# Products of the identity with itself behind the last value product of two head mixers

## The chip, the cores and the metric

The kernel runs on one core of a Trainium2 chip. The metric is the device time of one execution, in microseconds (us). Beside the median of several runs there is one profiled execution, whose trace gives the start and the length of every instruction on TensorE (PE; its weight loads are PEld), VectorE (DVE), ScalarE (ACT) and GpSimd (POOL), and the clock that was granted to TensorE: 1.00 stands for 2.4 GHz and 0.50 for 1.2 GHz.

## The reference, cut to what matters

Three layers run one behind another over 256 tokens of 1024 channels. Each layer has a mixer and a gated feed-forward part with a short convolution, and each of the two halves is entered through a modulated norm and left through a gated residual.

```python
for i in range(DEPTH):                       # two layers; a third has a mixer of its own
    sh1, sc1, g1, sh2, sc2, g2 = split(silu(c) @ ada_w[i] + ada_b[i])
    h = rms_norm(x, norm_mix[i]) * (1 + sc1) + sh1
    mix = stick_breaking_attention(h, ...) if i == 0 else dsa_attention(h, ...)
    x = x + g1 * mix
    h = rms_norm(x, norm_ffn[i]) * (1 + sc2) + sh2
    x = x + g2 * conv_ffn(h, ...)
...
o = einsum('bhqs,bshd->bqhd', a, v)          # the value product of a mixer, 16 heads of 64
return o.reshape(B, S, 1024) @ w_out         # and the product with its output weights
```

The change touches the end of the first two mixers: the value products of the last heads and what follows, the product with `w_out`, the residual and the entry into the feed-forward part.

## The kernel before, in words

All activations stand transposed, channels on the 128 partitions and 256 tokens along the free axis, in eight tiles of 128 channels. Large products are done in three terms: weights and activations are each split into a rounded part (`wh`, `xh`, `oh`) and a rest (`wl`, `xl`, `ol`), and `three` (L306) issues high times high, high times low and low times high into one PSUM bank. For weights, ScalarE makes `wh` (L412) out of the loaded `raw` and VectorE the rest `wl` (L424).

A mixer runs its heads as a background generator (`heads_in_flight`) between the pieces of the large products. For two heads at a time, `product(h)` issues a chain of four fp32 matmuls with 64 output columns (`po<-a,V` in the first mixer, `po<-pT,U` in the second); then `split_later` has ScalarE round the result to `oh` (L339) and VectorE subtract for `ol` (L340). The sixteen heads give eight channel tiles `k` of `oh` and `ol`.

`output` then multiplies by `w_out`. It goes through the first six tiles with `down`, as they come ready, and through the last two with `down_last`, which finishes the output tiles `m` in the order 0, 2, 4, 6, 1, 3, 5, 7. The eight output tiles share four `acc` banks, two to a bank: 0 and 1 share one, 2 and 3 the next. When an output tile is finished, `residual` has VectorE add it to `x` (L705, `x<-acc,mod,x`), ScalarE make the next half's `xh` out of it (L700), VectorE the rest `xl` (L701), and ScalarE and VectorE gather the squares for the next norm (`sq`, L650 and L731). The sums of squares are matmuls with a column of ones (`po<-ones,sq`). Between these stand VectorE's row products for the modulation of later layers (`ada_one`, L544, 1.2 us each), which wait for their weights `adaw` from memory, and, behind all of them, `opening`, the first product of the feed-forward part.

The order on each engine is set by a scheduler that simulates the program; a dependency without a semaphore (`behind`) ties one instruction behind another. `busy` (L897) issues fp32 products of a 128x128 tile of minus ones with itself into the `small` PSUM bank, read by nobody; the kernel before calls it three times at the start of the program (18, 8 and 8 products), and nowhere else.

In what follows, **the first place** is the end of the first mixer (`stick`, from 137 to 158 us of the span) and **the second place** the end of the second mixer (`sparse`, from 467 to 484 us).

Of the kernel before, what the change touches and what calls it, by code (L numbers as in the profile page):

```python
# [273 lines left out]
class Prog:  # L274
# [312 lines left out]
    def gate(self, L, h, k):  # L587
        return self.M[L][:, 6 * h + 4 + k // 4, k % 4:k % 4 + 1]
# [305 lines left out]
        nc.scalar.activation(self.ident_r, self.ident, AF.Copy)  # L894
        return p

    def busy(self, n):  # L897

        b = self.bank("small")
        for _ in range(n):  # L900
            self.mmul(b[:, 0:128], self.negones, self.negones, start=True, stop=True)

    def pin(self, mark):
        last = {}
# [121 lines left out]
    def stick(self, outer):  # L1026
        nc = self.nc
        with ExitStack() as es:
            pool = lambda name, bufs: es.enter_context(self.tc.tile_pool(name=name, bufs=bufs, reuse_waits="tile"))
            sv = pool("sbv", 3)  # L1030
            V = sv.tile([128, 2, D], F32, name="V", bufs=1)
            qk, ready, st = {}, set(), {}

            def value(i):
                def fn(u, b):
                    c = i * 512 + u * 256
                    nc.scalar.activation(V[:, :, c:c + 256], b, AF.Copy)
                return fn

            def heads(g):  # L1040
                def fn(u, b):
                    if u == 0:
                        qk[g] = sv.tile([128, 4, T], F32, name="qk")
                    nc.scalar.activation(qk[g][:, 2 * u:2 * u + 2], b, AF.Copy, scale=(0.125, 1.0)[u])
                    if u:
                        ready.add(g)
                return fn

            Z, S, E, PO = {}, {}, {}, {}

            def strict(w):

                d = w.rearrange("p (a t) -> p a t", a=3)[:, 0:3:2, :]
                return nc.gpsimd.affine_select(d, d, pattern=[[0, 2], [1, 128]], base=-1, channel_multiplier=-1,
                                               compare_op=ALU.is_ge, fill=0.0).ins

            def scores(h0, n):
                for h in range(h0, h0 + n):
                    Z[h] = self.score_bank(h, st)
                chain = []  # L1060
                for i, j in ((i, j) for i in range(2) for j in reversed(range(n))):
                    h = h0 + j
                    r = slice(h % 2 * 64, h % 2 * 64 + 64)
                    q, k = qk[h // 4][r, h % 4 // 2], qk[h // 4][r, 2 + h % 4 // 2]
                    chain.append(self.mmul(Z[h][:, i * 256:256 + i * 128], k[:, i * 128:i * 128 + 128], q[:, i * 128:256],
                                           start=i == 0))
                self.chained(chain)
                for h in range(h0, h0 + n):
                    soft(h)

            def soft(h):
                z = Z[h]
                e = sp.tile([128, 384], F32, name="e")
                nc.scalar.activation(e, z[:, :384], AF.Abs)
                self.act(e, e, AF.Exp, scale=-1.0)
                self.act(e, e, AF.Ln, bias=1.0)
                S[h] = sp.tile([128, 384], F32, name="s", bufs=4)

                def fn():
                    nc.vector.scalar_tensor_tensor(S[h], z[:, :384], 0.0, e, op0=ALU.max, op1=ALU.add)  # L1080
                    strict(S[h])
                self.after(1, fn)

            def suffix(h):
                z, s = Z.pop(h), S.pop(h)
                self.mmul(z[:, 0:256], self.nu, s[:, 0:256])
                self.mmul(z[:, 128:256], self.negones, s[:, 256:384])
                self.mmul(z[:, 256:384], self.nu, s[:, 256:384], stop=True)
                E[h] = sp.tile([128, 384], F32, name="a", bufs=WP + 1)
                self.act(E[h], z[:, :384], AF.Exp)  # L1090
                strict(E[h])

            def product(h):
                if h % 4 == 0:
                    PO[h // 4] = self.bank("po")
                o = PO[h // 4][:, h % 4 // 2 * 256:h % 4 // 2 * 256 + 256]
                a = [E.pop(h), E.pop(h + 1)]
                chain = []
                for t in range(2):
                    for i in (1, 0):  # L1100
                        r, c = slice(i * 64, i * 64 + 64), slice((h + i) * 64, (h + i) * 64 + 64)
                        chain.append(self.mmul(o[r, t * 128:256], V[:, t, c], a[i][:, t * 256:256 + t * 128],
                                               t == 0 and h % 4 == 0, t == 1))
                self.chained(chain)
                st["split"] += 1
                self.split_later(oh[:, h // 2], ol[:, h // 2], o,
                                 lambda: st.update(ready=h + 2, split=st["split"] - 1))

            self.start([value(0), heads(0), heads(1), value(1)], V, sv)
            sk, sp = pool("sbk", 1), pool("sb", 2)  # L1110
            bias = outer.enter_context(self.tc.tile_pool(name="bias", bufs=1, reuse_waits="tile", side="right"))
            bias = bias.tile([128, 16, 256], F32, name="bias")
            self.side.append(self.bias_tables(bias, pool("bk", 1)))
            oh = sk.tile([128, KT, T], F32R, name="oh")
            ol = sk.tile([128, KT, T], F32R, name="ol")
            self.bg.append(self.heads_in_flight(16, st, lambda h: h // 4 in ready, scores, suffix, product, 1, 2, 3))
            self.rate = RS[0]
            for g in (2, 3):
                for u in range(2):
                    self.unit(lambda b, g=g, u=u: heads(g)(u, b))  # L1120
            self.rate = RS[1]
            self.output(oh, ol, st, lambda k: st["ready"] > 2 * k + 1, 0)
            assert not self.side
            return bias

    def output(self, oh, ol, st, need, L, gate=lambda k: None):
        self.flush()
        st["hold"] = True
        while st["open"]:
            self.turnover()  # L1130
            self.advance()
        st["hold"], st["out"] = False, True
        if not LATE:
            self.ada_until(L, 5 if 2 * L + 1 == self.stage else 9)
        self.down_start()
        for k in range(KT - 2):
            while not need(k):
                self.turnover()
                self.advance()
            self.down(oh[:, k], ol[:, k], gate(k))  # L1140
        self.finish_bg()
        self.flush()
        if LATE:
            self.ada_until(L, 5 if 2 * L + 1 == self.stage else 9)
        self.down_last([(oh[:, k], ol[:, k]) for k in range(KT - 2, KT)], self.residual(L, 0))

    def transposed(self, sp, p, b):
# [26 lines left out]
    def sparse(self, bias):  # L1174
        nc, I = self.nc, self.I
        blocks = ((0, slice(0, 128)), (1, slice(128, 384)))
        with ExitStack() as outer:
# [23 lines left out]
            st = {}  # L1201
# [100 lines left out]
            Z, L, E, PO, asked = {}, {}, {}, {}, {}  # L1302
# [36 lines left out]
            def product(h):  # L1339
                if h % 4 == 0:  # L1340
                    PO[h // 4] = self.bank("po")
                o = PO[h // 4][:, h % 4 // 2 * 256:h % 4 // 2 * 256 + 256]
                pT = [E.pop(h), E.pop(h + 1)]
                chain = []
                for t in range(2):
                    for i in (1, 0):
                        r, c = slice(i * 64, i * 64 + 64), slice((h + i) * 64, (h + i) * 64 + 64)
                        rhs = pT[i][:, 128:256] if t else pT[i].rearrange("p (i t) -> p i t", i=3)[:, 0:3:2]
                        chain.append(self.mmul(o[r, t * 128:256], U[:, 1 - t, c], rhs, t == 0 and h % 4 == 0, t == 1))
                self.chained(chain)  # L1350
                st["split"] += 1
                self.split_later(oh[:, h // 2], ol[:, h // 2], o,
                                 lambda: st.update(ready=h + 2, split=st["split"] - 1))

            self.after(1, lambda: self.bg.extend(
                [index(), self.heads_in_flight(16, st, lambda h: h // 4 in ready, scores, turn, product, out_open=3)]))
            for g in range(4):
                if g == 2:
# [390 lines left out]
```

## Time and profile before

| | us |
|---|---|
| median of three runs | 1016.92 |
| lowest and highest of them | 1014.66, 1017.6 |
| the profiled execution | 1016.9 |
| its span, first to last instruction | 1014.9 |
| TensorE busy | 987.1 (97% of the span) |
| VectorE busy | 831.9 (82%) |
| ScalarE busy | 632.6 (62%) |
| mean granted clock of TensorE | 0.994 |

The span and the 2.0 us that lie outside it make the time. TensorE is busy nearly throughout, and by the chain of work that ended last 86% of the span is its. Matmuls overlap in the trace: one of 256 columns lasts 0.28 us while the next begins 0.12 us after it, so that durations of neighbours are not added; what counts is the distance of their starts. A bracket in a timeline row gives how long the engine stood idle before the row and what ended it.

### The profile page before, as it was taken

What the parts mean: (1) busy time and instruction counts of PE and PEld (TensorE: products, weight loads), DVE (VectorE), ACT (ScalarE), POOL (GpSimd) and SP (SyncE); (2) the same over time, 40 slices, a digit from 0 to 9 for tenths busy, and PEclk for the clock granted to TensorE, in tenths of its full rate; (3) what the DMA queues carried; (4) which work ended last, traced back from release to release, by engine and by line L of the source; (5) the groups of instructions that cost most, each with busy time, mean ns of one, the idle gap of its engine ahead of it and who ended that gap; (6) DMA issues with size and microseconds to landing.
All of it is one profiled execution on the core that took longest, in us unless ns stands there. A gap on an engine that the chain in (4) does not pass through costs nothing.

```text
span 1014.9 us, 20080 instructions
## 1 busy us (share of the span) xinstructions
PE 987.1 (97%) x8044; PEld 957.2 (94%) x8044; DVE 831.9 (82%) x1550; ACT 632.6 (62%) x1092; POOL 102.1 (10%) x181
## 2 busy tenths in 40 slices
PE   8999989999999999999999999999999999999997
PEld 8998879999999989988999999999988999999996
DVE  6987698999999899986898899877977689667654
ACT  5585648755554684886875555567785487445543
POOL 0026530011111010110000010100110000000000
PEclk9999999999999999999999999999999999999998
DMA  9999586688988285652668787827670346656531
GB/s 357 405 352 356 184 305 209 209 309 305 313 309 311 108 304 197 233 204 83 231 232 293 268 282 276 288 101 251 250 263 20 126 154 222 224 210 213 203 126 43
DMA packets 45934, 236.71 MB, mean 233 GB/s; under 512 B 5392, under 2 KB 5920, under 8 KB 28176
## 3 DMA queue, kind: packets, MB, share of 16 engines
q1 hardware_dynamic: 26064, 164.73, 44.9%
q0 software_dynamic: 19488, 70.31, 19.6%
q8 instruction: 63, 1.03, 0.4%
q10 hardware_dynamic: 288, 0.39, 0.1%
q14 instruction: 31, 0.25, 0.1%
HBM read 234.33 MB, written 1.07 MB: 232 GB/s over the span
## 4 chain that ended last, share of the span: by engine, by line
PE 86%; DVE 5%; ACT 4%; DMA 4%; issue 1%; SPq 0%; DVEq 0%; POOL 0%; ACTq 0%
PE mm L303 33%; PE acc L303 33%; PE small L303 10%; PE po L303 9%; DVE wl L424 1%; ACT wh L412 1%; DMA adaw<-ada 1%; DVE x L705 1%; DMA raw<-sb 1%; DVE adaw L544 1%; PE acc L1149 1%; DMA raw<-hg 1%; DVE xl L701 1%; DMA raw<-dsa 0%; DMA raw<-ffn 0%
## 5 line engine op out<-in xcount | busy, mean ns | idle before, releaser
L412 ACT ACTIVATE wh<-raw 128x1024 fp32r<-128x1024 f32 x290 | 304.9, 1057 | 255.2 <-PE acc L303 90.2
L424 DVE TENSOR_TENSOR wl<-raw,wh 128x1024 fp32r<-128x1024 f32 x290 | 353.2, 1224 | 92.5 <-ACT wh L412 91.6
L303 PE MATMUL mm<-xl,wh 128*128 128x256 f32 (+1 forms) x872 | 245.7, 283 | 1.2 <-DVE xl L701 1.2
L303 PE MATMUL mm<-xh,wh 128*128 128x256 f32 (+1 forms) x872 | 244.0, 285 | 1.3 <-DVE iv L1684 0.8
L303 PE MATMUL mm<-xh,wl 128*128 128x256 f32 (+1 forms) x872 | 244.6, 283 | 0.0
L544 DVE SCALAR_TENSOR_TENSOR adaw<-adaw,cond 128x1024 f32<-128x1024 f32 x144 | 176.1, 1226 | 6.9 <-DMA adaw<-ada 6.9
L303 PEld LDWEIGHTS mm<-xh,wh 128*128 128x128 f32 x872 | 163.3, 189 | 4.9 <-issue 1.7
L303 PEld LDWEIGHTS mm<-xl,wh 128*128 128x128 f32 x872 | 164.7, 189 | 2.8 <-DVE xl L701 1.8
L303 PEld LDWEIGHTS mm<-xh,wl 128*128 128x128 f32 x872 | 164.1, 189 | 0.2
L303 PE MATMUL acc<-gl,wh 128*128 128x256 f32 x528 | 148.1, 281 | 1.1 <-DVE gl L340 1.1
L303 PE MATMUL acc<-gh,wl 128*128 128x256 f32 x528 | 149.1, 283 | 0.0
L303 PE MATMUL acc<-gh,wh 128*128 128x256 f32 x528 | 148.3, 283 | 0.6 <-DVE x L705 0.6
L537 POOL DMA_DIRECT2D adaw<-ada x125 | 66.5, 532 | 717.2 <-DVE adaw L544 562.0
L303 PEld LDWEIGHTS acc<-gl,wh 128*128 128x128 f32 x528 | 100.3, 190 | 1.3 <-DVE gl L340 1.3
L303 PEld LDWEIGHTS acc<-gh,wh 128*128 128x128 f32 x528 | 98.8, 188 | 0.8 <-DVE x L705 0.8
L303 PEld LDWEIGHTS acc<-gh,wl 128*128 128x128 f32 x528 | 98.9, 187 | 0.0
L303 PE MATMUL small<-xh,wh 128*128 128x256 f32 x240 | 67.7, 282 | 0.0
L303 PE MATMUL small<-xh,wl 128*128 128x256 f32 x240 | 67.6, 282 | 0.0
L303 PE MATMUL small<-xl,wh 128*128 128x256 f32 x240 | 67.4, 281 | 0.0
L303 PE MATMUL acc<-ol,wh 128*128 128x256 f32 x192 | 55.4, 292 | 4.5 <-DVE ol L340 3.7
L303 PE MATMUL acc<-oh,wl 128*128 128x256 f32 x192 | 55.0, 291 | 0.0
L303 PE MATMUL po<-xh,wh 128*128 128x256 f32 x192 | 54.1, 282 | 0.0
(321 smaller groups left out, 2052.2 us busy)
## 6 DMA issues: line engine op xcount, KB each, us to landing
raw<-ffn SPq DMA_DIRECT2D x99, 1024.0 KB, 5.0
adaw<-ada POOLq DMA_DIRECT2D x125, 512.0 KB, 5.3
raw<-dsa SPq DMA_DIRECT2D x15, 1024.0 KB, 5.0
raw<-hg SPq DMA_DIRECT2D x15, 1024.0 KB, 4.9
adaw<-ada SPq DMA_DIRECT2D x19, 512.0 KB, 10.5
raw<-sb SPq DMA_DIRECT2D x16, 512.0 KB, 10.2
raw<-sb SPq DMA_DIRECT2D x8, 1024.0 KB, 8.1
bias<-scr POOLq DMA_DIRECT2D x8, 256.0 KB, 6.9
```

Of the source, the lines that this page charges most:

```text
L303: return self.nc.tensor.matmul(o, a, b, start=start, stop=stop, skip_group_check=True).ins
L412: inst = nc.scalar.activation(h[:, :k * n], self.raws[b][:, c0:c0 + k * n], AF.Copy).ins
L424: inst = nc.vector.tensor_tensor(l[:, :k * n], self.raws[b][:, c0:c0 + k * n], h[:, :k * n], op=ALU.subtract).ins
L537: self.nc.gpsimd.dma_start(raw, self.I[f"ada{L}"][b])
L544: return self.nc.vector.scalar_tensor_tensor(w, w, 1.0, self.cond, op0=ALU.mult, op1=ALU.mult, accum_out=self.M[n // 12][:, n % 12, k:k + ...
L701: return lambda: nc.vector.scalar_tensor_tensor(self.xl[:, m, 0:T], self.x[:, m], a, self.xh[:, m, 0:T], op0=ALU.mult, op1=ALU.subtract)
L705: self.lastx = nc.vector.scalar_tensor_tensor(self.x[:, m], o, self.gate(L, h, m), self.x[:, m], op0=ALU.mult, op1=ALU.add).ins
L1149: self.chained([nc.tensor.transpose(b[:, i * 128:(i + 1) * 128], p[:, i * 128:(i + 1) * 128], self.ident).ins for i in (1, 2, 0)])
```

## The change

`busy` can be given a tile other than the minus ones, and an instruction behind which all of its products are tied. In the first and the second mixer `product` keeps its last matmul in `st["last"]`. `output`, ahead of `down_last`, issues twelve products of the 128x128 fp32 identity with itself in layer 0 and seven in layer 1, tied behind that last matmul. The third mixer keeps no last matmul and gets none.

```diff
-    def busy(self, n):
+    def busy(self, n, w=None, behind=None):
         b = self.bank("small")
+        w = self.negones if w is None else w
         for _ in range(n):
-            self.mmul(b[:, 0:128], self.negones, self.negones, start=True, stop=True)
+            inst = self.mmul(b[:, 0:128], w, w, start=True, stop=True)
+            if behind is not None:
+                self.behind(inst, behind)
...
                 self.chained(chain)
+                st["last"] = chain[-1]
                 st["split"] += 1
...
             self.ada_until(L, 5 if 2 * L + 1 == self.stage else 9)
+        if "last" in st:
+            self.busy((12, 7)[L], self.ident, st["last"])
         self.down_last([(oh[:, k], ol[:, k]) for k in range(KT - 2, KT)], self.residual(L, 0))
```

On TensorE, at the first place, the rows `po<-a,V` are the value product of the last two heads, and `acc<-ol,wh` is the first matmul of `down_last`:

```order
 L303 MATMUL po<-a,V 64x256 x2
 L303 MATMUL po<-a,V 64x128 x2
+L303 MATMUL small<-ident 128x128 x12
 L303 MATMUL acc<-ol,wh 128x256
 L303 MATMUL acc<-oh,wl 128x256
```

The twelve products stand between the two; the order of the products with `w_out` around them is as it was.

On TensorE, at the second place, `mm<-ident,lg` are the transpositions of the last head's weights, `po<-pT,U` the last value product:

```order
 L303 MATMUL acc<-oh,wh 128x256 x4
-L1149 MATMUL mm<-ident,lg 128x128 x3
+L1155 MATMUL mm<-ident,lg 128x128 x3
 L303 MATMUL po<-pT,U 64x256 x2
 L303 MATMUL po<-pT,U 64x128 x2
+L303 MATMUL small<-ident 128x128 x7
 L303 MATMUL acc<-ol,wh 128x256
 L303 MATMUL acc<-oh,wl 128x256
```

Seven products stand there; the two rows with a minus and a plus are the same instruction under another line number.

On VectorE, at the first place, behind the four residuals of output tiles 0, 2, 4 and 6 (`x<-acc,mod_168,x`, L705; `xl`, L701, is the rest for the next half, `sq`, L731, adds up squares). Before:

```order
L705 SCALAR_TENSOR_TENSOR x<-acc,mod_168,x 128x256 x4
L570 TENSOR_TENSOR mod_168<-mod_168,vec 128x4
L701 SCALAR_TENSOR_TENSOR xl<-x,gain_171,xh 128x256 x2
L705 SCALAR_TENSOR_TENSOR x<-acc,mod_168,x 128x256
L701 SCALAR_TENSOR_TENSOR xl<-x,gain_171,xh 128x256 x2
L731 TENSOR_TENSOR sq<-sq 128x512
L705 SCALAR_TENSOR_TENSOR x<-acc,mod_168,x 128x256
L701 SCALAR_TENSOR_TENSOR xl<-x,gain_171,xh 128x256
L705 SCALAR_TENSOR_TENSOR x<-acc,mod_168,x 128x256 x2
L701 SCALAR_TENSOR_TENSOR xl<-x,gain_171,xh 128x256
```

And in the changed kernel, the same stretch of the same engine:

```order
L705 SCALAR_TENSOR_TENSOR x<-acc,mod_168,x 128x256 x4
L570 TENSOR_TENSOR mod_168<-mod_168,vec 128x4
L701 SCALAR_TENSOR_TENSOR xl<-x,gain_171,xh 128x256
L705 SCALAR_TENSOR_TENSOR x<-acc,mod_168,x 128x256
L701 SCALAR_TENSOR_TENSOR xl<-x,gain_171,xh 128x256
L705 SCALAR_TENSOR_TENSOR x<-acc,mod_168,x 128x256
L701 SCALAR_TENSOR_TENSOR xl<-x,gain_171,xh 128x256 x2
L705 SCALAR_TENSOR_TENSOR x<-acc,mod_168,x 128x256
L731 TENSOR_TENSOR sq<-sq 128x512
L705 SCALAR_TENSOR_TENSOR x<-acc,mod_168,x 128x256
```

The residuals of output tiles 1, 3 and 5 move ahead of rests and squares; the instructions are the same. In `opening` behind it, one group of three matmuls on TensorE changes places with two others. Everything else, on VectorE, ScalarE, GpSimd and the DMA queues, stands in the order of before.

## Rows read from the trace of the kernel before

**Rows 1.** The page, part 1: busy us, share of the span, instructions, by engine.

```profile
PE 987.1 (97%) x8044; PEld 957.2 (94%) x8044; DVE 831.9 (82%) x1550; ACT 632.6 (62%) x1092; POOL 102.1 (10%) x181
```

**Rows 2.** Windows at both places: stretch, length, busy by engine, PEclk, DMA share, GB/s.

```profile
139.83:142.70 2.87, 0.00 (x0) 0.00 (x0) 1.49 (x5) 1.06 (x1) 0.72 (x2) 1.00 1.00 368
142.70:142.99 0.29, 0.00 (x0) 0.00 (x0) 0.29 (x2) 0.02 (x1) 0.25 (x1) 0.50 0.88 357
142.99:146.11 3.12, 3.12 (x14) 3.12 (x15) 3.12 (x5) 0.37 (x1) 0.55 (x2) 0.50 0.90 335
146.11:154.32 8.21, 7.99 (x65) 7.57 (x63) 8.21 (x22) 6.13 (x13) 0.79 (x2) 1.00 0.39 133
...
470.38:470.77 0.39, 0.00 (x0) 0.00 (x1) 0.34 (x1) 0.02 (x1) 0.00 (x0) 0.50 0.19 42
470.77:473.79 3.02, 3.02 (x14) 3.02 (x15) 0.42 (x1) 0.36 (x1) 0.00 (x0) 0.50 0.00 0
473.79:479.52 5.73, 5.73 (x47) 5.45 (x46) 5.45 (x14) 4.47 (x11) 0.00 (x0) 1.00 0.00 0
```

**Rows 3.** Timeline of PE, first place: start, length, instructions, idle time before and releaser.

```profile
138.96 0.87 PE L303 MATMUL po<-a,V 128*64 128x256 f32 x8 [1.35 <-POOL a L1054]
142.99 0.58 PE L303 MATMUL acc<-ol,wh 128*128 128x256 f32 x1 [3.17 <-DVE ol L340]
...
147.14 0.39 PE L303 MATMUL acc<-oh,wh 128*128 128x256 f32 x1
...
154.69 0.39 PE L303 MATMUL mm<-xh,wh 128*128 128x258 f32 x1 [0.47 <-ACT wh L412]
...
155.28 0.95 PE L303 MATMUL po<-ones,sq 128*128 128x1 f32 x8
```

**Rows 4.** Timeline of PE, second place.

```profile
467.67 0.55 PE L1149 MATMUL mm<-ident,lg 128*128 128x128 f32 x3 [0.33 <-ACT lg L1329]
469.37 0.87 PE L303 MATMUL po<-pT,U 128*64 128x256 f32 x8 [1.16 <-ACT pT L1152]
470.77 0.58 PE L303 MATMUL acc<-ol,wh 128*128 128x256 f32 x1 [0.53 <-DVE ol L340]
...
473.71 0.32 PE L303 MATMUL acc<-oh,wl 128*128 128x256 f32 x1
...
475.07 0.28 PE L303 MATMUL acc<-oh,wh 128*128 128x256 f32 x1
...
476.02 0.28 PE L303 MATMUL acc<-oh,wl 128*128 128x256 f32 x1
```

**Rows 5.** Timeline of PE: products of minus ones at the start, a value product inside.

```profile
12.74 1.95 PE L303 MATMUL small<-negones 128*128 128x128 f32 x16
...
122.23 0.87 PE L303 MATMUL po<-a,V 128*64 128x256 f32 x8
123.04 0.38 PE L303 MATMUL acc<-oh,wh 128*128 128x256 f32 x1
```

**Rows 6.** The chain that ended last, first place: start, length, what.

```profile
144.41 2.29 DVE adaw L544 x4
146.69 1.57 DVE x L705 x4
```

**Rows 7.** Timeline of DVE, first place.

```profile
143.99 0.42 DVE L340 TENSOR_TENSOR ol<-po,oh 128x256 fp32r<-128x256 f32 x1
...
146.61 1.66 DVE L705 SCALAR_TENSOR_TENSOR x<-acc,mod,x 128x256 f32<-128x256 f32 x4
...
154.18 0.70 DVE L731 TENSOR_TENSOR sq<-sq 128x512 f32<-128x512 f32 x1
```

**Rows 8.** Timeline of ACT, first place.

```profile
151.34 0.51 ACT L700 ACTIVATE xh<-x,gain 128x256 fp32r<-128x256 f32 x1 [1.06 <-DVE x L705]
...
153.60 1.04 ACT L412 ACTIVATE wh<-raw 128x1024 fp32r<-128x1024 f32 x1
```

**Rows 9.** Timeline of DVE, second place.

```profile
471.17 0.42 DVE L340 TENSOR_TENSOR ol<-po,oh 128x256 fp32r<-128x256 f32 x1 [0.45 <-ACT oh L339]
474.07 1.66 DVE L705 SCALAR_TENSOR_TENSOR x<-acc,mod,x 128x256 f32<-128x256 f32 x4 [2.48 <-PE acc L303]
```

More of the change, by code (lines that the diff above doesn't have):

```diff
@@ L1350, in product @@
                 self.chained(chain)
+                st["last"] = chain[-1]
                 st["split"] += 1
```

## The prediction

> **What bounds the kernel now.** I read the page's part 1 first: TensorE (PE) is busy 97% of the span [rows 1], so the time is its work, its few waits, and its clock. Next came the granted clock, in ever smaller windows. Between the warm-up and the last microseconds it falls to 0.50 at just two places, and these are the two places of the change: from 142.70 to 146.11 us and from 470.38 to 473.79 us [rows 2]. What PE did before them differs: ahead of the first it stood idle for 3.17 us behind the value product, waiting for VectorE's `ol`; ahead of the second it had idled 0.33 and 1.16 us between transpositions and the value product, and the fall came within the last wait of 0.53 us [rows 3, 4]. At the lower level the matmuls of `down_last` start every (473.71 - 470.77) / 13 = 0.226 us, at the higher one every (476.02 - 475.07) / 8 = 0.119 us [rows 4]. Each fall thus costs PE about 3.4 us / 2 = some 1.6 us of work, 3.1 to 3.2 us for both, just over 0.3% of the time. Whether the 1.6 us reach the end is another matter, and the timelines of PE, VectorE (DVE) and ScalarE (ACT) at each place decide that.
>
> **The change part by part.** *Price of a product.* The nearest row is the eight products of minus ones at the start, same shape, same engine: 16 matmuls in 1.95 us [rows 5]. With the last matmul lasting some 0.28 us, as its neighbours do, that is (1.95 - 0.28) / 15 = 0.111 us a matmul, 0.22 us a product at the higher clock, and by the ratio of the two levels an estimated 0.44 us at the lower. A value product of eight matmuls gives PE free 0.81 us after its start (122.23 to 123.04) [rows 5].
>
> *First place, twelve products.* They begin at 138.96 + 0.81 = 139.77 and end after 12 x 0.22 = 2.67 us, at 142.44. `ol` comes at 142.99, so 0.55 us of wait are left and nothing is delayed: the wait that hides them is 3.17 us long, and it is VectorE's, which the change does not touch. With PE working up to 142.44 in place of idling from 139.83, I expect the clock to stay at 1.00. What does that give back? In the chain, PE does not appear from there until 154.69: VectorE's two row products run to 146.61, and the residuals of output tiles 0, 2, 4, 6 follow at once [rows 6, 7]. PE's part of them was ready before VectorE was, even at half clock. PE's second half (tiles 1, 3, 5, 7, in the same banks) can only begin when VectorE has read the first: 147.14 in the row, 0.5 us behind VectorE's start, and at that time the clock was back at 1.00 anyway [rows 2, 3]. So of the 1.6 us of the first fall I count nothing: PE finishes early and waits longer for VectorE.
>
> *VectorE's order at the first place.* The residuals of tiles 1, 3 and 5 now stand ahead of rests and squares. In the trace ACT waits 1.06 us for such a residual at 151.34, and the weights it rounds behind that, at 153.60, are what PE waits 0.47 us for at 154.69 [rows 3, 8]. An earlier residual brings ACT and so PE forward, by 0.47 us at most; next late is the sum of squares, where VectorE's total work is unchanged: its last square ends at 154.18 + 0.70 = 154.88 and PE's sums start at 155.28 [rows 3, 7]. That leaves 0 to 0.40 us. I take 0.35, near the upper end, since ACT's wait of 1.06 us is over twice the wait that it has to cover.
>
> *Second place, seven products.* Here PE sets the end: VectorE waits 2.48 us for it, up to 474.07 [rows 9]. The products begin at 469.37 + 0.81 = 470.18 and take 7 x 0.22 = 1.56 us, to 471.74, if the clock holds. That is 0.97 us later than `down_last` starts now, at 470.77 [rows 4]: only 0.53 us of wait was there to be filled. From then on the 14 matmuls up to the first residual go at the faster pace: 13 x 0.119 + 0.28 + 0.04 = 1.87 us, so the residual starts at 473.61 against 474.07. Gain: 0.46 us. The last `ol` is there at 471.17 + 0.42 = 471.59 and delays nothing [rows 9]. If the clock falls at 470.38 all the same, one product is done by then and six take 0.44 us each: `down_last` starts at 473.04, does three steps until 473.79 and ten more at the fast pace, and the residual starts at 473.79 + 10 x 0.119 + 0.32 = 475.30. Loss: 1.2 us. I take the gain. The rows bear this way: ahead of the first place's value product PE idled 1.35 us at a stretch and the clock stayed at 1.00 for another 2.9 us [rows 2, 3], while the longest idle stretch ahead of the second fall is 1.16 us, and the 0.53 us within which the clock fell are now filled. They do not settle it: the fill begins only 0.2 us ahead of that fall.
>
> *Nothing else moves.* The `small` bank is free at both places, nobody reads it, and its next writer is PE itself.
>
> *Sum*, against the profiled execution (span 1014.9 us and 2.0 us around it, 1016.9, which is also the median of the runs shown): 1016.9 - 0.35 - 0.46 = 1016.1 us.
>
> **The rivals.** *The second fall stays.* The 0.55 us of PE work shortly before that fall are transpositions [rows 4]. If such work does little for the clock, and 0.2 us of products come too late, the fall stays and the products stand in its way: +1.2 - 0.35 = +0.85, 1017.8 us. For it: the fall in the trace came 3.2 us after the last dense stretch, with real work in between. Against it: the longer idle stretch at the first place that the clock survived. The Trainium skill, page "TensorE: Matmul & The Clock Gate", section "Part 4: PE-mode transpose", says that transpositions do not count as activity for the clock in the way that matmuls do. By that rule this rival is the likelier; the trace agrees with it in so far as the fall followed transpositions, and shows no case that separates the two.
>
> *The first fall moves (slower).* At full clock PE does the 20 matmuls of the first half in 2.4 us, to 145.4, and then idles until VectorE lets it go on at 147.14: a new wait of some 1.7 us, longer than the 1.35 that the clock survived, shorter than the 2.87 us before it fell [rows 2, 3]. If the clock now falls as PE takes up the second half, the cost lands where PE is busy to 154.3: 15 steps until the clock is back, 0.107 us more each, 1.6 us, less the 0.47 us that PE waits at 154.69 anyway, so 1.1 us, and the 0.35 are lost. With the second place's gain: 1016.9 + 1.1 - 0.46 = 1017.5 us. It decides when the new wait is long enough; VectorE's row products, which wait for weights from memory, set its length.
>
> *Both falls were on the path.* If the first fall's 1.6 us did reach the end, by way of what PE hands over at 146 to 147 us, the sum would be 1016.9 - 1.6 - 0.46 = 1014.8 us. The row speaks against it: VectorE did not wait for PE at 146.61 [rows 7].
>
> *The cover differs.* In an execution in which the clock holds at the second place already, the products cost plainly what they overrun: 1.0 us, less 0.35, 1017.5 us. Nothing in one trace shows how often that is.
>
> *Something else shifts.* Any new order meets other landings of transfers; I have no row that prices it.
>
> **How the numbers follow.** Forecast 0.40 (1016.1); the second fall stays 0.20 (1017.8); the first fall moves 0.13 (1017.5); the cover differs 0.07 (1017.5); both falls on the path 0.08 (1014.8); something else 0.12, half of it on each side beyond 3 us. A measurement of this kernel can tell about 0.3% from no change, some 3.1 us; all the priced cases lie within that. So faster by more than 0.3%: 0.06; within: 0.88; slower: 0.06. The range takes in 1014.8 at the lower end and, at the upper, 1017.8 and part of the case in which both bad turns meet (1016.9 + 1.1 + 1.2 = 1019.2): 1014.6 to 1018.6 us.
>
> **What would show it.** In the trace of the changed kernel: no stretch at 0.50 between the first value product and 154 us; PE idle for some 0.5 us ahead of `down_last` at the first place and for some 1.7 us in the middle of it, waiting for VectorE's residual, which starts as long after the value product as now; ACT's wait for a residual near 151 us and PE's wait for ACT near 154.6 us shorter. At the second place the seven products in about 1.6 us, no wait behind them, the clock at 1.00, and the first residual 4.2 us after the start of the value product against 4.7 now (474.07 - 469.37). The prediction is wrong if the clock falls at either place, if the twelve products take over 3.2 us and push `down_last` back, or if VectorE waits for PE at the first place.

## The result, and the profile after

| | before | after |
|---|---|---|
| median of five runs each | 1015.16 | 1020.33 |
| lowest and highest | 1014.66, 1017.6 | 1019.66, 1022.83 |
| the profiled execution | 1016.9 | 1020.3 |
| its span | 1014.9 | 1018.3 |

The changed kernel takes 1.0053 times as long, with an interval of 1.0041 to 1.0065: 5.2 us slower. That is outside the range of the prediction and on the side that had 0.06. The five runs of the kernel before contain the three of the prediction, whose median was 1016.92.

Part 1 and two lines of part 3 of the page of the changed kernel (queue and kind, packets, MB, share of 16 engines), which answer to [rows 1]:

```profile
PE 990.9 (97%) x8082; PEld 960.9 (94%) x8082; DVE 832.5 (82%) x1550; ACT 632.7 (62%) x1092; POOL 104.6 (10%) x181
...
q1 hardware_dynamic: 26064, 164.73, 44.5%
...
q8 instruction: 63, 1.03, 0.4%
```

TensorE is busy 3.8 us longer, with 38 more matmuls and 38 more loads. Nothing here looks like trouble. The last line, which the page of before has too, word for word, will turn out to be the one that I should have read.

**The first place** went as forecast. Windows of the changed kernel: stretch, length, busy by engine (PE, PEld, DVE, ACT, POOL), PEclk, DMA share, GB/s (against [rows 2]):

```profile
139.01:141.70 2.69, 2.69 (x26) 2.69 (x24) 1.75 (x8) 1.27 (x2) 1.61 (x3) 1.00 0.88 312
142.10:144.71 2.61, 2.61 (x20) 2.40 (x20) 2.59 (x5) 0.29 (x1) 0.20 (x1) 1.00 0.94 330
144.71:146.28 1.57, 0.00 (x0) 0.00 (x1) 1.57 (x4) 0.02 (x1) 0.69 (x2) 1.00 0.91 352
146.28:153.50 7.22, 6.77 (x54) 6.57 (x55) 7.22 (x19) 6.48 (x13) 0.38 (x1) 1.00 0.47 157
```

Timeline of PE there (against [rows 3]):

```profile
138.20 0.87 PE L303 MATMUL po<-a,V 128*64 128x256 f32 x8 [0.93 <-POOL a L1057]
139.00 2.94 PE L303 MATMUL small<-ident 128*128 128x128 f32 x24
...
146.28 0.39 PE L303 MATMUL acc<-oh,wh 128*128 128x256 f32 x1 [1.57 <-DVE x L705]
...
154.44 0.95 PE L303 MATMUL po<-ones,sq 128*128 128x1 f32 x8
```

The twelve products fill the idle stretch, the granted clock stays at 1.00, and PE idles for 1.57 us in the middle of `down_last`, waiting for VectorE. The first row stands 0.76 us earlier than in [rows 3], the last one 0.84 us: the first place yields 0.1 us and costs nothing.

**The second place** is where it was lost. Timeline of PE, against [rows 4]:

```profile
467.04 0.55 PE L1155 MATMUL mm<-ident,lg 128*128 128x128 f32 x3 [0.41 <-ACT lg L1335]
470.43 1.55 PE L303 MATMUL po<-pT,U 128*64 128x256 f32 x8 [2.83 <-ACT pT L1158]
471.90 3.36 PE L303 MATMUL small<-ident 128*128 128x128 f32 x14
474.91 0.56 PE L303 MATMUL acc<-ol,wh 128*128 128x256 f32 x1
```

And its windows, against [rows 2]:

```profile
467.59:469.80 2.21, 0.00 (x0) 0.00 (x0) 0.00 (x0) 0.86 (x1) 0.00 (x0) 1.00 0.00 0
469.80:470.43 0.63, 0.01 (x1) 0.01 (x1) 0.40 (x1) 0.57 (x2) 0.00 (x0) 0.50 0.00 0
470.43:471.97 1.54, 1.54 (x9) 0.83 (x9) 0.82 (x1) 0.00 (x0) 0.00 (x0) 0.50 0.00 0
471.97:474.91 2.94, 2.94 (x15) 2.94 (x15) 0.85 (x2) 0.38 (x1) 0.00 (x0) 0.50 0.00 0
474.91:476.63 1.72, 1.72 (x10) 1.72 (x10) 0.00 (x0) 0.00 (x0) 0.00 (x0) 0.50 0.00 0
```

The transpositions stand 0.63 us earlier than before, but PE then waits 2.83 us for `pT` where it had waited 1.16. During that wait the clock falls, at 469.80, before the value product has even begun and with it any of the products that were to hold it. The value product takes 1.54 us in place of 0.81, the seven products 2.94 us, all on the path, and `down_last` starts 474.91 - 470.77 = 4.14 us later than before. From the delay of the value product come 1.06 us, from its half pace 0.73, and from the products 2.94 less the 0.59 us between 470.18 and 470.77 that were PE's free time and wait before, 2.35 in all. The first residual is 3.55 us late, 477.62 in the timeline of VectorE against 474.07 in [rows 9], and the span is 3.4 us longer:

```profile
477.62 1.66 DVE L705 SCALAR_TENSOR_TENSOR x<-acc,mod,x 128x256 f32<-128x256 f32 x4 [4.30 <-PE acc L303]
```

Why is `pT` late? Timeline of ACT, of the changed kernel and behind it of the kernel before:

```profile
468.94 1.06 ACT L412 ACTIVATE wh<-raw 128x1024 fp32r<-128x1024 f32 x1 [1.95 <-DMA raw<-ffn]
469.90 0.47 ACT L1158 ACTIVATE pT<-mm 128x384 f32<-128x384 f32 x1
```

```profile
467.89 1.06 ACT L412 ACTIVATE wh<-raw 128x1024 fp32r<-128x1024 f32 x1 [0.28 <-DMA raw<-ffn]
468.85 0.47 ACT L1152 ACTIVATE pT<-mm 128x384 f32<-128x384 f32 x1
```

ACT works in order, and ahead of `pT` stands the rounding of weights for the feed-forward part. It waits for their transfer: 1.95 us against 0.28. The transfer, in the chain of after (start, length, what), answers to one of 463.07 and 4.73 us in the chain of before:

```profile
462.37 6.48 DMA raw<-ffn
```

It was issued 0.70 us earlier and landed 1.05 us later. So the question for the runs is why a transfer of the same size, in the same order on its queue, takes 1.75 us more.

### The profile page after: what moved, and what is told of

It reads as the page before. It is cut to its first block, busy times and chain, and to the rows that moved or that the text cites. A ratio compares the mean times of both kernels' runs of the same rounds, so it can differ in the third digit from the quotient of the medians.

```text
span 1018.3 us, 20155 instructions
## 1 busy us (share of the span) xinstructions
PE 990.9 (97%) x8082; PEld 960.9 (94%) x8082; DVE 832.5 (82%) x1550; ACT 632.7 (62%) x1092; POOL 104.6 (10%) x181
## 3 DMA queue, kind: packets, MB, share of 16 engines
q8 instruction: 63, 1.03, 0.4%
## 4 chain that ended last, share of the span: by engine, by line
PE 87%; DVE 5%; DMA 3%; ACT 3%; issue 1%; SPq 0%; DVEq 0%; POOL 0%; ACTq 0%
PE mm L303 34%; PE acc L303 33%; PE small L303 10%; PE po L303 10%; DVE wl L424 1%; DVE x L705 1%; ACT wh L412 1%; DMA adaw<-ada 1%; DVE xl L701 1%; DMA raw<-sb 1%; DVE adaw L544 1%; DMA raw<-hg 1%; DMA raw<-ffn 1%; PE acc L1155 1%; DMA raw<-dsa 0%
## 5 line engine op out<-in xcount | busy, mean ns | idle before, releaser
L303 PE MATMUL acc<-oh,wh 128*128 128x256 f32 x192 | 52.1, 291 | 2.5 <-DVE x L705 1.6
```

The source lines that it names most:

```text
L303: return self.nc.tensor.matmul(o, a, b, start=start, stop=stop, skip_group_check=True).ins
```

## The experiments

Theories for the first group of runs. **A**: the loss is the seven products themselves, at half clock on the path. **B**: the first place is done earlier, and that shifts later transfers. After that group two more took the place of B. **C**: TensorE's own program comes over the same DMA engines, in blocks; 48 added instructions (24 matmuls and 24 loads) move each later fetch ahead by some 3 us, and one of them into the tail of this transfer. **D**: it is the work at the first place, its order on VectorE and the earlier start of what follows, that delays the transfer. Edits are shown against the changed kernel; where several lines with a plus bear names, each is the edit of the run named. Ratios are to the kernel before on the same chip, over all runs; they need not be the quotient of the two medians, which stand beside them. The expectations of a group stand behind its edits, run by run.

**Neither place, first alone, second alone, and the second ahead of the value product.**

```diff
-            self.busy((12, 7)[L], self.ident, st["last"])
+            self.busy((0, 0)[L], self.ident, st["last"])      # e3_none
+            self.busy((12, 0)[L], self.ident, st["last"])     # e1_first_only
+            self.busy((0, 7)[L], self.ident, st["last"])      # e2_second_only
```

For e5_ahead the products of the second place are tied behind the last transposition and stand ahead of the value product:

```diff
-            self.busy((12, 7)[L], self.ident, st["last"])
+            self.busy((12, 6)[L], self.ident, (st["last"], getattr(self, "turned", None))[L])
...
+        self.turned = turned[-1]       # in transposed(): the last of the three transpositions
```

Expected of e3_none, e1_first_only, e2_second_only and e5_ahead, in this order:

> The changed code with no products at either place (0 and 0); every engine's order is that of before. Theory A (the loss of some 5 us is the seven products at the second place, run at half clock where TensorE sets the end) and theory B (the earlier end of the first place shifts the later transfers, so that the weights ahead of the second place's last value product land later): both expect the time of before, within 1 us. Its trace is a second look at before: A expects TensorE's wait ahead of the last value product of the second mixer to vary by itself between 1.2 and some 2.8 us, B expects 1.2 us as in the first trace.

> Twelve products at the first place, none at the second. Theory A: 0.4 to 1 us faster than before (the 0.75 us that the first place brought in the trace of after). Theory B: about 1 us slower than before (0.75 us gained, 1.7 us lost on the later landing), with a wait of some 2.8 us ahead of the last value product of the second mixer.

> No products at the first place, seven at the second. Theory A: 2.5 to 5 us slower than before, nearly all of the loss of after and 0.4 to 1 us more; the seven products last 2.9 us in the trace where the clock is at 0.50 and 1.6 us where it is at 1.00. Theory B: slower by no more than 2.7 us, with the wait ahead of the value product 1.2 us as in before.

> Twelve products at the first place; at the second place six, tied behind the last transposition and so ahead of the last value product, in the wait for the transposed weights, none behind it. Theory A: TensorE waits there anyway, so the six products (1.3 us at full clock) cost nothing and the clock stays up over the value product and the first matmuls behind: 1 to 2.5 us faster than before. Theory B: the landing is late because of the first place, so no better than before (0 to 1 us slower).

Measured: e3_none 1016.52 us against 1015.51, ratio 1.0017 [1.0002, 1.0032]. Its engines run the same instructions in the same order as before, so this is how far two equal kernels can stand apart here, and nothing below 0.2% is read as an effect from here on. e1_first_only 1018.84, 1.0040 [1.0028, 1.0052]; e2_second_only 1016.53, 1.0020 [1.0004, 1.0036]; e5_ahead 1016.08, 1.0009 [0.9993, 1.0024]. Against the expectations: e1 is 3.3 us slower than before where A had it faster and B 1 us slower; e2 is 1.0 us above before, where A wanted 2.5 at least; e5 came out as B had it.

The same transfer, in the chain of e1_first_only (start, length, what):

```profile
462.57 5.96 DMA raw<-ffn
```

in that of e2_second_only:

```profile
461.86 4.75 DMA raw<-ffn
```

in that of e3_none:

```profile
461.86 4.74 DMA raw<-ffn
```

and in that of e5_ahead:

```profile
462.16 6.38 DMA raw<-ffn
```

With the twelve products the transfer is late, without them it is not, and the seven products have no say in it. Theory A falls as the whole cause: the second place alone, 1016.53, is no slower than the control e3, 1016.52. But it holds a part. Timeline of PE in e1:

```profile
470.10 0.87 PE L303 MATMUL po<-pT,U 128*64 128x256 f32 x8 [2.33 <-ACT pT L1158]
```

and in e2:

```profile
468.19 0.87 PE L303 MATMUL po<-pT,U 128*64 128x256 f32 x8 [1.08 <-ACT pT L1158]
468.99 3.00 PE L303 MATMUL small<-ident 128*128 128x128 f32 x14
```

In e2 the clock fell too, at 469.4, for 3.4 us, and its first residual came 5.92 us after the value product's start against 4.70 before. That difference is 1.2 us, what I had priced for this case. In e3 the clock happened to hold there, with no product at all, and the residual came after 3.35 us: the fall at this place cost 4.70 - 3.35 = 1.35 us in before. In e5 the products keep PE busy during the wait, as its timeline shows:

```profile
467.21 1.50 PE L303 MATMUL small<-ident 128*128 128x128 f32 x12
470.11 0.87 PE L303 MATMUL po<-pT,U 128*64 128x256 f32 x8 [1.40 <-ACT pT L1160]
```

The value product starts as late as in e1, but the clock stays at 1.00 there, and nearly the whole loss is gone. Theory A had it faster than before; it is the same within the interval.

**What moves the transfer: the work at the first place, or the number of instructions.** f4_start_only has twelve more products at the start of the program and none elsewhere; f2_fetch_back has twelve at the first place and twelve fewer at the start; f1_six_first has half. f3_wide keeps PE busy with a quarter of the instructions.

```diff
-        self.busy(18)
+        self.busy(30)        # f4_start_only, with (0, 0)
+        self.busy(6)         # f2_fetch_back, with (12, 0)
...
+            self.busy((6, 0)[L], self.ident, st["last"])      # f1_six_first
+            self.busy((3, 1)[L], self.ident, (st["last"], getattr(self, "turned", None))[L])   # f3_wide
...
+                self.behind(self.mmul(b, w, self.vec[:, 0:512], start=True, stop=True), behind)   # f3_wide, in busy()
```

Expected of f1_six_first, f2_fetch_back, f4_start_only and f3_wide, in this order:

> Six products at the first place, none at the second; VectorE's order at the first place is that of after. Theory C (TensorE's program is fetched in blocks over the same DMA engines; the 48 instructions of twelve products bring each later fetch some 3 us earlier, and the one that then falls into the tail of the weight transfer ahead of the second place's last value product delays its landing): six products move the fetch half as far, to about 468.5 us, behind the landing, so the transfer takes 4.7 to 4.8 us as in before, TensorE waits 1.1 to 1.2 us for the value product, and the time is within 1 us of before. Theory D (the landing is late because of what the first place now does: VectorE's order and the earlier start of what follows): the transfer takes 6 us or more, and the time is 2 to 4 us above before.

> Twelve products at the first place, none at the second, and twelve fewer (6 for 18) of the products at the start of the program, so that the first place is followed by the same number of instructions up to each fetch as in before. Theory C: the fetch is back at about 470 us and the transfer takes 4.7 to 4.8 us; the time is that of before but for what the start loses on a clock that rises later. Theory D: the transfer still takes 6 us or more.

> Nothing at either place, but twelve more (30 for 18) of the products at the start of the program: the same 48 instructions, far from both places. Theory C: the fetch stands at about 467 us plus what the start loses, and the transfer ahead of the second place's last value product takes 6 to 6.5 us, with a wait of 2.3 to 2.9 us; slower than before by 1.7 us and up to 2.7 us that the products take at the start. Theory D: the transfer takes 4.7 to 4.8 us.

> Another fill of the same length with a quarter of the instructions: three products of 512 columns (the constants' tile against the identity) behind the first mixer's last value product, and one behind the last transposition of the second mixer, none behind its value product. Theory C: the fetch moves by some 0.7 us only and the transfer takes 4.7 to 4.8 us; with the clock held at both places 1 to 2 us faster than before. Theory D: the transfer takes 6 us or more, and the time is that of the six products ahead of the value product (0.6 us above before).

Measured, against 1016.07: f1 1016.16, 0.9998 [0.9985, 1.0010]; f2 1018.67, 1.0017 [1.0004, 1.0030]; f4 1024.58, 1.0085 [1.0070, 1.0100]; f3 1015.53, 0.9998 [0.9988, 1.0008]. The totals of f2 and f4 hold what was done to the start of the program as well, so the transfer is the measure here. f4 lost 8.5 us, about twice the most that I had expected: in its profiled execution the transfer is issued 5.0 us later than in before, and at the first place the clock was at 0.50 for 13.7 us (141.33 to 154.99), against 3.4 in before. f3 is not the 1 to 2 us faster that I had expected. DMA view of f4, of the stretch in which the transfer runs (queue and kind, packets, MB, share; then the issues with KB and us to landing):

```profile
q1 hardware_dynamic: 195, 1.34, 51.6%
q8 instruction: 1, 0.02, 0.8%
...
raw<-ffn SPq DMA_DIRECT2D x1, 1024.0 KB, 6.4
```

And of f2:

```profile
q1 hardware_dynamic: 208, 1.44, 62.9%
...
raw<-ffn SPq DMA_DIRECT2D x1, 1024.0 KB, 4.8
```

These two decide between C and D. f4 has nothing at the first place, the same order there as before, and the transfer is late, though all the work comes later and not earlier, against B. f2 has all twelve products there and it is on time: 4.85 us. What the late ones share is a packet of the queue `q8 instruction` inside the transfer's time; f2's window has none. Theories B and D fall.

**The changed kernel again, fewer instructions at both places, and the second place alone, ahead of the value product.**

```diff
+            self.busy((3, 2)[L], self.ident, st["last"])      # g1_wide_both, busy() as in f3_wide
+            self.busy((0, 5)[L], self.ident, (st["last"], getattr(self, "turned", None))[L])   # g3_second_ahead
```

Expected of g2_after_again (the changed kernel, no edit), g1_wide_both and g3_second_ahead, in this order:

> The changed kernel once more, beside the next run on the same chip. 4 to 6 us slower than before; in the trace the transfer ahead of the second place's last value product takes 6 us or more with a program fetch in its tail, TensorE waits 2.3 to 2.9 us, and the seven products take 1.6 us or, after a fall of the clock, up to 3 us.

> The change with its fill made of fewer instructions: three products of 512 columns at the first place and two at the second, each behind the last value product as in the change (12 and 8 instructions of TensorE for 48 and 28, filling 2.6 and 1.7 us). Theory C (most of the loss is the fetch that the extra instructions move into the transfer): the transfer takes 4.7 to 4.8 us, the products behind the value product still overrun their wait by some 1 us, and the time is within 1.5 us of before. Theory A (the loss is the products at the second place): 3 to 5 us slower than before, as the changed kernel.

> No products at the first place; five at the second, tied behind the last transposition, ahead of the value product, none behind it. Theory C: the fetch stays where it is in before, the transfer takes 4.7 to 4.8 us, the five products (1.1 us) fit the wait of 1.1 to 1.2 us and the clock holds over value product and down_last: 0.5 to 1.5 us faster than before. Theory A: the same. It is the version that the experiments point to; a gain under 1 us would not be told from no change.

Measured, against 1016.51: g2 1019.73, 1.0039 [1.0023, 1.0054]; g1 1016.59, 1.0010 [0.9993, 1.0027]; g3 1014.74, 0.9980 [0.9964, 0.9995]. The changed kernel loses 3.2 us here, less than the 5.2 at first and than the 4 to 6 that I had expected. g1 stands at the same places as the change and covers PE nearly as long: at the second place its two products of 512 columns hold PE for 2.61 us (471.77 to 474.38), mostly at half clock, against 3.01 for the seven in after. It does so with a quarter of the instructions, and its transfer takes 4.80 us.

```profile
471.77 3.60 PE L303 MATMUL small<-vec,ident 128*128 128x512 f32 x4
474.38 1.18 PE L303 MATMUL acc<-ol,wh 128*128 128x256 f32 x1
```

So the loss of the change goes with the number of instructions, not with the filling of the wait.

g3 is the lowest of all. Its timeline of PE at the second place:

```profile
467.48 1.28 PE L303 MATMUL small<-ident 128*128 128x128 f32 x10
468.85 0.87 PE L303 MATMUL po<-pT,U 128*64 128x256 f32 x8
```

And its windows:

```profile
467.60:468.85 1.25, 1.16 (x12) 0.97 (x10) 0.40 (x1) 1.19 (x2) 0.00 (x0) 1.00 0.05 13
468.85:472.21 3.36, 2.83 (x24) 2.45 (x25) 1.67 (x3) 0.38 (x1) 0.00 (x0) 1.00 0.00 0
```

Five products fit the wait, the value product starts without a bracket, the clock is 1.00 throughout and the residual follows after 3.36 us, 1.34 less than before. By its interval it is 0.2% faster than the kernel before, and its median is 5.0 us below that of the changed kernel on this chip (g2). Since two equal kernels stood 0.17% apart above, I call the place mended and the gain in time likely, not settled.

**The clock over all runs.** At the first place it falls between 139 and 143 us in the five profiled executions that have no products there (before, e2, e3, f4, g3), and in none of the eight that have some; f3 has a later fall, told below. At the second place it falls in all four with products behind the value product (after, g2, g1, e2), in none of the three with products ahead of it (e5, f3, g3), and of those with none at that place it falls in three (before, e1, f4) and holds in three (e3, f1, f2). So g3's held clock alone would prove little. Nor do all four of the first kind count: in after and g2 the fall came in the long wait, ahead of the value product and of every product behind it, and only in e2 and g1 did the fill behind the value product come too late. The three kinds together point to a fill ahead as the better one; with one profiled execution of each kernel they do not settle it. Elsewhere in the span the clock fell too, for 3.4 us at 10.9 us in f1 and g3 and at some 666 us in e3 and f1.

**All runs at the second place.** "Took" is the transfer from issue to landing; "fetch" is when the packet of q8 starts, counted from that issue; "wait" is PE's, ahead of the value product; the last column is from the start of the value product to that of the first residual. All in us, from the profiled executions.

| kernel | products at start, first, second | took | fetch | wait | to residual |
|---|---|---|---|---|---|
| before | 18, 0, 0 | 4.73 | 7.5 | 1.16 | 4.70 |
| e3_none | 18, 0, 0 | 4.74 | 7.3 | 1.10 | 3.35 |
| e2_second_only | 18, 0, 7 | 4.75 | 7.5 | 1.08 | 5.92 |
| after | 18, 12, 7 | 6.48 | 4.5 | 2.83 | 7.19 |
| g2_after_again | 18, 12, 7 | 6.58 | 4.4 | 2.88 | 5.75 |
| e1_first_only | 18, 12, 0 | 5.96 | 3.5 | 2.33 | 4.31 |
| e5_ahead | 18, 12, 6 ahead | 6.38 | 4.4 | 1.40 | 3.36 |
| f4_start_only | 30, 0, 0 | 6.44 | 4.4 | 2.82 | 5.48 |
| f2_fetch_back | 6, 12, 0 | 4.85 | 7.4 | 1.23 | 3.36 |
| f1_six_first | 18, 6, 0 | 4.95 | 4.4 | 1.34 | 3.36 |
| f3_wide | 18, 3 wide, 1 wide ahead | 4.72 | 5.7 | 0.27 | 3.36 |
| g1_wide_both | 18, 3 wide, 2 wide | 4.80 | 5.8 | 1.24 | 6.19 |
| g3_second_ahead | 18, 0, 5 ahead | 4.86 | 6.2 | 0.09 | 3.36 |

Five kernels have the long transfer, and in all five the fetch comes 3.5 to 4.5 us after the issue, when the transfer is in its last packets; where the fetch comes 5.7 us or more after the issue, the transfer has landed. f1 is the odd one: I expected its fetch some 2 us later than it came, and it came at the critical time and did no harm. The single packets show why. The transfer ends with 16 small packets of 4 bytes, which I read as the end of one of 16 shares each; in the trace's records of packets they and the fetch stand so:

| kernel | last but one small packet | fetch starts | fetch ends | next packet of the transfer | last small packet |
|---|---|---|---|---|---|
| after | 466.78 | 466.83 | 467.75 | 467.74 | 467.74 |
| e5_ahead | 466.47 | 466.52 | 467.44 | 467.43 | 467.43 |
| f4_start_only | 472.49 | 472.52 | 473.47 | 473.46 | 473.46 |
| g2_after_again | 466.94 | 467.01 | 467.96 | 467.94 | 468.73 |
| e1_first_only | 466.89 | 466.07 | 467.04 | 467.03 | 468.11 |
| f1_six_first | 466.50 | 466.50 | 467.46 | 466.66 | 466.66 |

In the five late ones a packet of the transfer starts within 0.02 us of the fetch's end: one share of the transfer stood in line behind the 16 KB of instructions, for 0.92 to 0.97 us, while the other 15 came to their end. No record names the DMA engine of a packet; that the two share one is read from these times. No other queue than `q1` and `q8` moved a packet while the transfer ran, in any of the thirteen kernels. In f1 the transfer's packets were all under way or done, and none follows the fetch. The landing comes 0.36 to 0.44 us after the last small packet in before, e1, f1 and g2, but 1.06 to 1.11 us after it in after, e5 and f4; that further 0.7 us no record explains.

The rest of the span says the same. In the packet records of the thirteen profiled executions, 373 transfers of 1 MB were issued by SyncE when its earlier ones had landed or were within 0.3 us of it, and had no packet of `q0` in their time. (The transfer of the second place is not among them, since an earlier one is under way for its first 1.2 us or more.) The 203 without a fetch in their time took 4.6 to 5.1 us, every one. Of the 21 in which a fetch started 1.0 to 4.0 us after the issue, 20 took 5.7 to 6.4 us. Of the 94 in which it started 4.0 to 5.0 us after the issue, at the very end, 93 took 4.6 to 5.2 us. (In the other 55 it started earlier than 1.0 us, and they took 4.7 to 7.4.) So a fetch amid a transfer makes it late, and one at its end mostly does no harm, as in f1. And a late landing costs nothing where nobody waits for it: the next transfer of these weights, issued at 483.9 us in f1 and at 484.2 in g3, had a fetch inside and took 7.07 and 7.14 us, no engine waited for it, and neither kernel is slower than before.

## Why the prediction was wrong

**The step that failed** is "Nothing else moves". I looked there for other writers of a PSUM bank, and in the order of the instructions for what changes its place; the instructions that are added were given a price on PE and none as a program. The number to have worked with stood on the page: 63 packets of `q8 instruction`, 1.03 MB, thus 16.3 KB each, for 2 x 8044 instructions of PE [rows 1], 255 to a packet and a packet every 1014.9 / 63 = 16.1 us. The twelve products are 24 matmuls and 24 loads, 48 of 255, so at an even pace, as an estimate, every later fetch comes 48 / 255 x 16.1 = 3.0 us earlier against the work. The one at the second place starts 7.5 us after the transfer's issue before and 4.5 after. Before, the fetch had come 2.8 us behind the landing, and that margin was used up.

The Trainium skill, page "Runtime: NRT & Kernel Launch", section "Instruction fetch mechanics", says that an engine's instructions are streamed in blocks of 16 KiB or 256 instructions over a DMA queue of its own, and that the cost of a new block is mostly hidden. The size and the count agree with the trace. The cost was not in TensorE's own supply of instructions here: it fell on a data transfer, by 0.9 us of standing in line behind the fetch and a landing 1.2 to 1.8 us later.

That q8 carries TensorE's program rests on that count and on f2 beside e1 and f4 beside e3, which differ in the number of PE's instructions ahead of the place and, in the first 41 us alone, in some order of VectorE, ScalarE and the DMA issues; no record names the engine that a fetch is for.

**Second place: the clock.** I took the gain, that the products hold the clock, and it fell. The term went wrong before its own condition came up: the wait of 1.16 us that I carried over became 2.83, and the fill stands behind the value product, where it cannot shorten a wait ahead of it. In e2, where the wait was 1.08, the clock fell as well, at 469.4, some 0.4 us after the products had begun; so in that execution the fill came too late even with the transfer on time. The rival "the second fall stays" was the better choice; its price, +1.2 us, is what e2 shows against before. It was too small for after, since there the value product ran at half clock too and the products stayed at 0.42 us each from first to last. The rule of the Trainium skill on transpositions (page "TensorE: Matmul & The Clock Gate", section "Part 4: PE-mode transpose"), cited with that rival, is not settled: g3 holds the clock with products in the same wait, but no run fills it with transpositions.

**Price of a product.** Right: 2.94 / 12 = 0.245 us with the last one's tail at the first place, against 0.22 forecast, and 2.94 / 7 = 0.42 at half clock, against 0.44.

**First place.** Right in the main steps: no fall, the new wait of 1.57 us (1.7 forecast), VectorE not waiting for PE. The idle 0.55 us ahead of `down_last` had shrunk to 0.09: the products ended at 139.00 + 2.94 = 141.94 and `down_last` began at 142.03, so the cover was nearly used up. The 0.35 us from VectorE's order are not to be found: 0.1 us by the rows above. ACT's wait did shrink, from 1.06 to 0.48 us, and PE's wait for `wh` is gone, but PE then waits 0.45 us for an `xl` that it had not waited for. The rival "the first fall moves" is real, though not in this execution: in the profiled one of f3, with three wide products at the first place, the clock was at 0.50 from 150.20 to 153.60, in the second half of `down_last`, just as described. The rival "both falls on the path" has nothing for it.

**Range and chances.** "Something else shifts" is what happened. It had 0.12, half to each side, for want of a row, and it lay outside the range by its own words. With the row of q8, and with ACT waiting 0.28 us for this transfer already before, it had a place, a price (one packet's time on one engine, then PE's wait and the fall) and a condition, and it would have been a rival of the first order.

**Order of size.** The profiled executions differ by 3.4 us, the medians by 5.2. The 1.8 us between the two figures is the kernel before: its profiled execution, 1016.9, lies 1.7 us above the median of its five runs, while that of after is its own median. Executions of one program differ: those of e3 run from 1014.4 to 1022.6 us, and the clock falls at different places (e3's profile shows none at the second place, that of before does). The size of the loss is therefore known roughly: 5.2 us at first, 3.2 us with g2.

**Open.** In after the clock stayed at 0.50 for 6.8 us (469.80 to 476.63), though PE had work without a break from 470.43; in g2, the same program, it was 3.4 us from 470.4. No run here tells why. Nor is it shown how exactly a fetch's time follows from the count. The even pace is too simple: by it f1's 24 instructions would have moved the fetch 1.5 us, and they moved it 3.1, as far as 48 did, so that the 3.0 us for after are in part luck. The three fetches ahead of this one start 3.3, 5.9 and 4.7 us earlier in after than in before, of which the work itself has some 0.7. PE's waits stretch the pace: in before, e3 and f2 the fetch starts in PE's wait behind the value product, in f1, after, g2, e5 and f4 in its wait for `lg` ahead of the transpositions. By the records that is 22 instructions of PE earlier in the program but some 3 us earlier in time, with the wait for `pT` between the two.

## What to carry to other kernels

Added instructions are also added program: estimate how far they move every later block of it, and see which transfer that an engine waits for lands with less margin than that. By e5, f3 and g3 a fill belongs where the engine waits, ahead of the work that follows the wait and sized to the shortest wait seen, not behind that work; and it is better made of few long instructions, as g1 beside g2 shows. Where an engine already waits for a transfer, even briefly, price what happens if it lands a microsecond later.

## What the hardware showed that I had not expected

- At the second place a fetch of 16 KB of instructions held up one share of a 1 MB transfer for 0.92 to 0.97 us, and the transfer, which is over only when all 16 shares are, landed 1.2 to 1.8 us later in five kernels (6.0 to 6.6 us against 4.7 to 5.0 in the eight others). Elsewhere in the span 20 of 21 transfers with a fetch amid them took 5.7 to 6.4 us, and all 203 without one 4.6 to 5.1.
- Twelve products of no use at the start of the program, some 460 us ahead (f4), were followed by the same late landing, 6.44 us, as twelve at the first place (5.96 to 6.58).
- Products of no use held the granted clock at 1.00 through the idle stretch of the first place in all eight kernels that had them there, but in after, once it had fallen, 2.94 us of them ran at 0.50 without a break.
